# A two-layer decoder step on one core: order of copies and casts, a fourth place for down weights, and the second mixer's norm sum

## The chip, the core and the metric

The kernel runs on one core of a Trainium2 chip. Its time is the device time of one execution in microseconds, as the median of several runs. TensorE multiplies, VectorE and ScalarE do elementwise work and read the accumulators, GpSimd does elementwise work in SBUF, and SyncE issues most transfers from memory.

## The reference, cut to what matters

The reference computes one inference step of two decoder layers, in float32, for 512 prompt tokens and 64 sample tokens that share all weights (576 columns here):

```python
for l in range(2):
    y = mixer(rmsnorm(h, norm_mix[l]))       # layer 0: retention and gMLP; layer 1: windowed attention with sinks
    h = h + y
    h = h + square(relu(rmsnorm(h, norm_mlp[l]) @ w_up[l])) @ w_down[l]
y = rmsnorm(h, norm_final)
```

The width is 1024, that of the MLP 4096. Layer 1's mixer starts with `z = rmsnorm(h) @ w_qkv + b_qkv`: keys and values of 128 rows each, queries of 1024. New caches and states are outputs as well.

## The kernel before, in words

**Layout.** Activations lie transposed: `h[0..7]` are eight tiles of 128 rows by 576 columns. Every float32 product is made of three products of fp32r parts: each operand is split into a high part (a cast on ScalarE, `whi` for weights, line 248) and a low part (a subtraction on VectorE, `wlo`, line 259), and TensorE adds high x high, high x low and low x high in one accumulator. Norm operands are split in the same way (`xhi` line 395, `xlo` line 396). A chunk of 128 output rows is 48 matmuls of 288 columns each (`block`, line 304).

**Weights.** SyncE loads them in pieces of 128 x 1024 floats in a fixed `order`, into three places `raw` (`load_to`, line 215). `jobs` lists what is cast and in which order; `parts` are the finished pairs, for which there are six places (`NW_`). `ahead_to(n)` (line 272) casts until `n` jobs are prepared, and at its end calls `load_to(done + 3)`: three pieces beyond the last one whose casts are all issued.

**MLP.** `rounds_of` (line 434) goes through the 4096 hidden rows in four rounds of eight chunks. The up phase makes eight chunks; their squares are put into a tile `q` in pairs (one place, 128 x 2304 floats), combined there and split into `ahi`, `alo` (lines 475 to 486). The last VectorE instruction that reads `q` is the second subtraction of the fourth pair. The down phase has four *units* (`down_unit`, line 497), m = 0 to 3, each for two tiles of `h`. A unit is a block product with seven multiplications in place of eight (P1 to P7, 12 matmuls each, line 316), so weights are combined first: `s1 = a21 + a22`, `s2 = s1 + a11`, `s3 = a21 + a11`, `s4 = s2 + a12` on VectorE (line 233). A unit's weights are two pieces: `a11, a12` and `a21, a22`. Unit 0 runs P1, P2, P3, P5, P6, P4, P7, the others P1, P5, P6, P2, P7, P3, P4. Results are kept apart by copies on ScalarE: after P1 its bank is copied to `y` before P6 adds to it (line 552), after P6 to `z` (558), after P7 to `w` (565). The last round of the second layer has no units. So there are four rounds with units in the first MLP and three in the second. In the last round of the first, the next norm's operands and squares for finished tiles of `h` are made between the products (`nxt.chunk`, line 387); the squares (ScalarE, line 405) are added up on GpSimd (line 411).

```python
run("P1", x, True)              # takes its weights, multiplies, then ahead_to(used + 5)
y = bank("y")
nc.scalar.copy(out=y, in_=x)
f = bank("f")
run("P5", f, True)
shared(f)
run("P6", x, False)
```

**Order.** VectorE and ScalarE run the MLP in the order in which the program issues it (`manual_schedule`, line 429); elsewhere the compiler orders them. Each engine works through its own queue in order.

**The second mixer** (line 945). The key chunk is multiplied, then `norm.finish()` splits the sum of squares and lets TensorE add it over the partitions (lines 374, 375); the reciprocal root `rstd` scales the key chunk at its evacuation (line 969). The value chunk follows, then eight query chunks. There are two accumulators for chunks.

Of the kernel before, what the change touches and what calls it, by code (L numbers as in the profile page):

```python
# [11 lines left out]
F32 = mybir.dt.float32  # L12
# [6 lines left out]
P = 128  # L19
# [23 lines left out]
NW_ = 6  # L43
# [77 lines left out]
def hybrid_step(ctx: ExitStack, tc: tile.TileContext, a, o):  # L121
# [25 lines left out]
    nc.scalar.activation(out=warm, in_=eps_r, func=AF.Abs_reciprocal_sqrt)  # L147
    cols = keep.tile([P, NCOL], F32, name="cols")
    nc.scalar.dma_start(out=cols, in_=a["cols"])
    h, first = [], []  # L150
    for c in range(KC):
        t = keep.tile([P, T], F32, name=f"h{c}")
# [26 lines left out]


    jobs = [(("left", "right")[j], i) for i in range(len(order)) for j in range(2)]

    def add_pieces(aps):
        for ap in aps:
# [3 lines left out]
    def add_unit(pair, first):  # L188
        jobs.extend((n, len(order)) for n in (FIRST_UNIT if first else UNIT))
        order.extend(pair)  # L190

    def mlp_order(l, last):
        up, dn = a[f"w_up{l}"], a[f"w_dn{l}"]
        for r in range(32 // FB):
            add_pieces([up[r * FB + f] for f in range(FB)])
            if last and r == 32 // FB - 1:
                add_pieces([dn[r, c // 2, c % 2] for c in range(KC)] * 2)
            else:
                for m in range(KC // 2):
                    add_unit([dn[r, m, i] for i in range(2)], m == 0)  # L200

    mlp_order(0, False)
    add_pieces([w_qkv[j] for j in (8, 9, 0, 1, 2, 3, 4, 5, 6, 7)])
    add_pieces([a["w_o1"][c] for c in range(KC)])
    mlp_order(1, True)

    raws, parts, owed = [], [], []
    used, done, summed = [0], [0], [0]
    sums, sum_pool = {}, [None]

# [3 lines left out]

    def load_to(n):
        while len(raws) < min(n, len(order)):
            raw = wp.tile([P, 1024], F32, name="raw", tag="raw", bufs=3)
            nc.sync.dma_start(out=raw, in_=order[len(raws)].rearrange("p k c -> p (k c)"))
            raws.append(raw)

    def blocks_of(i):
        load_to(i + 2)
# [49 lines left out]
    def ahead_to(n):  # L272

        n = min(n, len(jobs))
        while len(parts) < n or owed:
            while summed[0] < min(len(parts) + 2, len(jobs)):
                job, i = jobs[summed[0]]
                k = SUMS.get(job)
                if k:
                    total(k, i)  # L280
                summed[0] += 1
            if len(parts) < n:
                prepare()
            split_low()
        load_to(done[0] + 3)

    def take(n):
        i = used[0]
# [33 lines left out]
    def gemm(xs, outs=None, sides=(0, 1), mid=None, ahead=1):  # L322

        n = len(xs)
        view = None
        if outs is None:
            acc = acc_tile()
            outs, view = [acc[:, hf, 0:TH] for hf in range(2)], acc[:, :, 0:TH]
        got = pieces(n // 8, ahead)
        for k in range(n):  # L330
            for fn in (mid or {}).get(k, ()):
                fn()
            block(outs, cut(got, k), xs[k], sides, k == 0, k == n - 1)
        return view
# [99 lines left out]
    def rounds_of(norm, nxt, mp):  # L434
        rounds = 32 // FB

        def up():

            acc, got = acc_tile(), take(2)
            for k in range(KC):  # L440
                block([acc[:, hf, 0:TH] for hf in range(2)], cut(got, k), norm.xs[k], (0, 1), k == 0, k == KC - 1)
            ahead_to(used[0] + NW_ - 2)
            return acc[:, :, 0:TH]

        def flat(v):
            return v.rearrange("p a b -> p (a b)")

        for r in range(rounds):
            plain = nxt is None and r == rounds - 1
            acts = []  # L450
            for p in range(FB // 2):

                q = mp.tile([P, 8, TH], F32, name="q", tag="q", bufs=1)
                hi = mp.tile([P, 7, TH], F32R, name="ahi", tag="ahi", bufs=FB // 2)
                lo = mp.tile([P, 7, TH], F32R, name="alo", tag="alo", bufs=FB // 2)
                for j in range(2):
                    view = up()
                    if r == 0 and p == 0 and j == 0:
                        norm.finish()
                    t = mp.tile([P, T], F32, name="t", tag="t")  # L460
                    nc.vector.scalar_tensor_tensor(out=halves(t), in0=view, scalar=0.0, in1=norm.rv,  # L461
                                                   op0=ALU.max, op1=ALU.mult)
                    if not plain and p == FB // 2 - 1 and j == 1:
                        ahead_to(used[0] + NW_ - 1)
                    seg = slice(2 * j, 2 * j + 2)
                    nc.scalar.activation(out=flat(q[:, seg]), in_=t, func=AF.Square)  # L466
                    if plain:
                        nc.scalar.activation(out=flat(hi[:, seg]), in_=t, func=AF.Square)  # L468
                        nc.gpsimd.tensor_tensor(out=lo[:, seg], in0=q[:, seg], in1=hi.bitcast(F32)[:, seg],  # L469
                                                op=ALU.subtract)  # L470
                        acts.append((flat(hi[:, seg]), flat(lo[:, seg])))
                if plain:
                    continue

                def two(s0, s1):
                    nc.scalar.copy(out=hi[:, s0 - 1:s1 - 1], in_=q[:, s0:s1])  # L476
                    nc.vector.tensor_tensor(out=lo[:, s0 - 1:s1 - 1], in0=q[:, s0:s1],  # L477
                                            in1=hi.bitcast(F32)[:, s0 - 1:s1 - 1], op=ALU.subtract)

                b12, b11, b22, b21, t1, t2, t3, t4 = (q[:, i] for i in range(8))  # L480
                nc.vector.tensor_tensor(out=t1, in0=b11, in1=b12, op=ALU.subtract)
                nc.vector.scalar_tensor_tensor(out=t2, in0=t1, scalar=-1.0, in1=b22, op0=ALU.mult, op1=ALU.subtract)
                nc.vector.tensor_tensor(out=t3, in0=b22, in1=b12, op=ALU.subtract)
                nc.vector.scalar_tensor_tensor(out=t4, in0=t2, scalar=-1.0, in1=b21, op0=ALU.mult, op1=ALU.subtract)  # L484
                two(1, 4)
                two(4, 8)
                acts.append((hi, lo))
            if plain:
                return [acts[2 * p + j] for j in range(2) for p in range(FB // 2)]
            between = []  # L490
            for m in range(KC // 2):
                down_unit(acts, m, m == 0, between, nxt)
                between = [2 * m, 2 * m + 1] if r == rounds - 1 else []
            for c in between:
                nxt.chunk(c)

    def down_unit(acts, m, first, between, nxt):

# [7 lines left out]
        def bank(name):  # L506
            return m_tile(name)[:, 0:TH]

        def run(n, out, start, stop=True, ks_=range(4), w=None, ahead=NW_ - 1):
            w = w or take(1)[0]  # L510
            product(out, w, lambda k: [t[:, operand[n]] for t in acts[k]], ks_, start, stop, m == KC // 2 - 1)
            if ahead:
                ahead_to(used[0] + ahead)

        def to_h(row, cols_, src, op):
            nc.vector.tensor_tensor(out=row[:, cols_], in0=row[:, cols_], in1=src, op=op)  # L516
# [5 lines left out]
        if first:  # L522
# [24 lines left out]
            to_h(row2, n1, z, ALU.subtract)  # L547
            to_h(row2, n2, z, ALU.subtract)
            return
        run("P1", x, True)  # L550
        y = bank("y")
        nc.scalar.copy(out=y, in_=x)  # L552
        f = bank("f")
        run("P5", f, True)
        shared(f)
# [10 lines left out]
        to_h(row2, n2, z, ALU.subtract)  # L566
        for c in between[1:2]:
            nxt.chunk(c)
        run("P3", x, False)
        to_h(row1, n2, x, ALU.add)  # L570
        run("P4", w_, False)
        to_h(row2, n1, w_, ALU.subtract)

    def last_block(acts, mp):

# [369 lines left out]
    def mixer1(norm, nxt):  # L945
        with tc.tile_pool(name="mx1", bufs=2) as mp:
# [11 lines left out]
            nc.sync.dma_start(out=o["ck_s"][:, 0:W - DL, :], in_=a["cache_k"][:, DL:W, :])  # L958
            nc.sync.dma_start(out=o["cv_s"][:, 0:W - DL, :], in_=a["cache_v"][:, DL:W, :])
            bq = cols[:, COL["b_qkv"]:COL["b_qkv"] + 10]  # L960
            bq8 = mp.tile([P, KC], F32, name="bq8", bufs=1)
            nc.vector.tensor_scalar(out=bq8, in0=bq[:, 0:KC], scalar1=SCALE_S, scalar2=None, op0=ALU.mult)
            xs = norm.xs
            rows_of = [slice(0, 64), slice(64, 128)]

# [3 lines left out]
                nc.vector.tensor_tensor(out=halves(z), in0=view, in1=norm.rv, op=ALU.mult)  # L969
                return z  # L970

            view = gemm(xs)
            norm.finish()
            kT = scaled(view)
            nc.scalar.activation(out=kT, in_=kT, func=AF.Identity, bias=bq[:, 8:9])

            kst = [[w(f"k{part}{kv}", F32R)[:, 0:NP] for part in "hl"] for kv in range(2)]
            for kv, kr in enumerate(rows_of):
                for ds_ in rows_of:
                    nc.scalar.copy(out=kst[kv][0][ds_], in_=kT[kr, 0:NP])  # L980
                own = kst[kv][0].bitcast(F32)
                for ds_ in rows_of:
                    nc.gpsimd.tensor_tensor(out=kst[kv][1][ds_], in0=kT[kr, 0:NP], in1=own[kr], op=ALU.subtract)
            vt = w("vt")[:, 0:NP].rearrange("p (n c) -> p n c", n=NB)
            kvs = mp.tile([NS, 2, P], F32, name="kvs", bufs=1)
            vs = kvs[:, 0, :]
# [21 lines left out]

                later(1, tokens)

            chunk(xs, v_out)


            qs = mp.tile([P, DB, KC, DL], F32, name="qs", bufs=1)
# [332 lines left out]
```

## Time and profile before

| | us |
|---|---|
| median of 3 runs | 1234.64 |
| lowest, highest | 1233.05, 1236.55 |
| the profiled execution | 1236.07 |
| its span, first to last instruction | 1234.0 |
| TensorE busy with matmuls | 1199.2 (97%) |
| VectorE busy | 854.1 (69%) |
| ScalarE busy | 582.3 (47%) |
| GpSimd busy | 192.2 (16%) |
| mean granted clock of TensorE | 0.991 |

Times within the profile count from the span's first instruction. Matmuls are pipelined: one is recorded for about 0.29 us, while in a full stream another starts every 0.13 us. A wait is put down to what released it last. In the rows PE is TensorE's matmuls, DVE VectorE, ACT ScalarE, POOL GpSimd, and SPq SyncE's DMA queue; `out<-in` are the kernel's tiles, and a merged row has a count (x4).

### The profile page before, as it was taken

What the parts mean: (1) busy time and instruction counts of PE and PEld (TensorE: products, weight loads), DVE (VectorE), ACT (ScalarE), POOL (GpSimd) and SP (SyncE); (2) the same over time, 40 slices, a digit from 0 to 9 for tenths busy, and PEclk for the clock granted to TensorE, in tenths of its full rate; (3) what the DMA queues carried; (4) which work ended last, traced back from release to release, by engine and by line L of the source; (5) the groups of instructions that cost most, each with busy time, mean ns of one, the idle gap of its engine ahead of it and who ended that gap; (6) DMA issues with size and microseconds to landing.
All of it is one profiled execution on the core that took longest, in us unless ns stands there. A gap on an engine that the chain in (4) does not pass through costs nothing.

```text
span 1234.0 us, 22717 instructions
## 1 busy us (share of the span) xinstructions
PE 1199.2 (97%) x9213; PEld 1180.0 (96%) x9213; DVE 854.1 (69%) x1546; ACT 582.3 (47%) x1101; POOL 192.2 (16%) x166
## 2 busy tenths in 40 slices
PE   8999999999999999999999999999999999999996
PEld 8999999999999999999999999999999999999996
DVE  8867785456856866875886778546785784784555
ACT  6333454444534444444455777444443443443363
POOL 3543340110000000000014553210000000001223
PEclk9999999999999999999999999899999999999998
DMA  8243222222242233142233212122233233123243
GB/s 281 89 137 122 73 75 83 86 69 72 83 120 70 69 120 86 52 138 69 58 97 110 67 39 67 52 72 71 64 116 90 66 94 113 54 86 120 86 154 111
DMA packets 38521, 113.62 MB, mean 92 GB/s; under 512 B 4161, under 2 KB 11521, under 8 KB 38401
## 3 DMA queue, kind: packets, MB, share of 16 engines
q1 hardware_dynamic: 37408, 110.31, 29.0%
q8 instruction: 72, 1.18, 0.4%
q0 software_dynamic: 320, 1.31, 0.3%
q10 hardware_dynamic: 688, 0.55, 0.2%
q14 instruction: 33, 0.26, 0.1%
HBM read 107.12 MB, written 6.03 MB: 92 GB/s over the span
## 4 chain that ended last, share of the span: by engine, by line
PE 81%; DVE 9%; ACT 3%; DMA 3%; issue 3%; SPq 0%; DVEq 0%; POOL 0%; ACTq 0%
PE acc L304 54%; PE acc L316 7%; PE dn L304 4%; DVE wlo L259 3%; PE w L316 3%; PE f L316 3%; PE y L316 2%; DMA raw<-in_w_dn 2%; PE z L316 2%; DVE h L516 1%; DVE s L233 1%; PE tpp L1093 1%; PE op L1106 1%; PE g L316 1%; ACT whi L248 1%
## 5 line engine op out<-in xcount | busy, mean ns | idle before, releaser
L304 PE MATMUL acc<-xhi,whi 128*128 128x288 f32 x1520 | 325.8, 296 | 0.3 <-DVE vz L708 0.3
L304 PE MATMUL acc<-xlo,whi 128*128 128x288 f32 x1520 | 322.7, 294 | 1.2 <-DVE xlo L396 1.2
L304 PE MATMUL acc<-xhi,wlo 128*128 128x288 f32 x1520 | 323.2, 294 | 0.0
L259 DVE TENSOR_TENSOR wlo<-raw,whi 128x512 fp32r<-128x512 f32 x340 | 250.1, 748 | 92.9 <-ACT whi L248 91.0
L248 ACT CAST whi<-raw 128x512 fp32r<-128x512 f32 x340 | 203.4, 619 | 160.4 <-PE acc L304 110.8
L304 PEld LDWEIGHTS acc<-xlo,whi 128*128 128x128 f32 x1520 | 243.1, 188 | 1.6 <-DVE xlo L396 1.6
L304 PEld LDWEIGHTS acc<-xhi,whi 128*128 128x128 f32 x1520 | 242.1, 188 | 1.8 <-issue 1.3
L304 PEld LDWEIGHTS acc<-xhi,wlo 128*128 128x128 f32 x1520 | 243.5, 188 | 0.3
L466 ACT ACTIVATE q<-t 128x576 f32<-128x576 f32 x64 | 43.9, 686 | 230.9 <-DVE t L461 230.9
L411 POOL TENSOR_TENSOR ssq<-ssq,sq 128x576 f32<-128x576 f32 x25 | 37.2, 1488 | 509.6 <-ACT sq L405 509.4
L461 DVE SCALAR_TENSOR_TENSOR t<-acc,rstd 128x576 f32<-128x576 f32 x64 | 48.4, 756 | 86.0 <-PE acc L304 85.7
L248 ACT CAST whi<-s 128x512 fp32r<-128x512 f32 x112 | 66.1, 620 | 73.4 <-DVE s L233 57.9
L259 DVE TENSOR_TENSOR wlo<-s,whi 128x512 fp32r<-128x512 f32 x112 | 75.7, 686 | 13.5 <-ACT whi L248 13.5
L316 PE MATMUL acc<-ahi,whi 128*128 128x288 f32 x308 | 65.6, 298 | 7.5 <-ACT y L552 7.5
L477 DVE TENSOR_TENSOR alo<-q,ahi 128x864 fp32r<-128x864 f32 (+1 forms) x56 | 67.5, 1205 | 7.2 <-ACT ahi L476 7.2
L316 PE MATMUL acc<-ahi,wlo 128*128 128x288 f32 x308 | 65.0, 296 | 0.0
L316 PE MATMUL acc<-alo,whi 128*128 128x288 f32 x308 | 64.8, 295 | 0.0
L476 ACT CAST ahi<-q 128x864 fp32r<-128x864 f32 (+1 forms) x56 | 58.2, 1039 | 11.9 <-DVE q L484 11.0
L469 POOL TENSOR_TENSOR alo<-q,ahi 128x576 fp32r<-128x576 f32 x8 | 11.5, 1434 | 328.2 <-ACT ahi L468 328.2
L233 DVE TENSOR_TENSOR s<-raw 128x512 f32<-128x512 f32 x56 | 40.9, 730 | 30.4 <-DMA raw<-in_w_dn 30.4
L316 PEld LDWEIGHTS acc<-ahi,whi 128*128 128x128 f32 x308 | 49.0, 189 | 9.3 <-ACT y L552 9.2
L316 PEld LDWEIGHTS acc<-ahi,wlo 128*128 128x128 f32 x308 | 49.1, 189 | 0.0
(323 smaller groups left out, 2213.3 us busy)
## 6 DMA issues: line engine op xcount, KB each, us to landing
raw<-in_w_dn SPq DMA_DIRECT2D x72, 512.0 KB
raw<-in_w_up SPq DMA_DIRECT2D x64, 512.0 KB
raw<-in_w_in SPq DMA_DIRECT2D x22, 512.0 KB
raw<-in_w_o SPq DMA_DIRECT2D x16, 512.0 KB
raw<-in_w_qkv SPq DMA_DIRECT2D x10, 512.0 KB
h<-in_xT SPq DMA_DIRECT2D x8, 288.0 KB
s<-in_s SPq DMA_DIRECT2D x4, 512.0 KB
out_ret_s<-s SPq DMA_DIRECT2D x4, 512.0 KB
```

Of the source, the lines that this page charges most:

```text
L233: nc.vector.tensor_tensor(out=sums[k, i], in0=x, in1=b[y], op=ALU.add)
L248: nc.scalar.copy(out=hi, in_=src)
L259: nc.vector.tensor_tensor(out=lo, in0=src, in1=hi.bitcast(F32), op=ALU.subtract)
L304: nc.tensor.matmul(out, lhsT=w_, rhs=x_[:, hf if isinstance(hf, slice) else half(hf)], start=(start and si == 0), stop=(stop and si == 2))
L316: nc.tensor.matmul(out, lhsT=w[wi][:, k * P:(k + 1) * P], rhs=x(k)[xi], start=(start and n == 0), stop=(stop and n == len(steps) - 1), ski ...
L411: nc.gpsimd.tensor_tensor(out=self.ssq, in0=self.ssq, in1=sq, op=ALU.add)
L461: nc.vector.scalar_tensor_tensor(out=halves(t), in0=view, scalar=0.0, in1=norm.rv, op0=ALU.max, op1=ALU.mult)
L466: nc.scalar.activation(out=flat(q[:, seg]), in_=t, func=AF.Square)
L476: nc.scalar.copy(out=hi[:, s0 - 1:s1 - 1], in_=q[:, s0:s1])
L477: nc.vector.tensor_tensor(out=lo[:, s0 - 1:s1 - 1], in0=q[:, s0:s1], in1=hi.bitcast(F32)[:, s0 - 1:s1 - 1], op=ALU.subtract)
L516: nc.vector.tensor_tensor(out=row[:, cols_], in0=row[:, cols_], in1=src, op=op)
L1093: nc.tensor.transpose(out=tp[:, i * P:(i + 1) * P], in_=s[:, n, hf * P:(hf + 1) * P], identity=ident)
```

## The change

- In unit 1 (m = 1) P1 casts nothing ahead; the copy to `y` follows it, and then `ahead_to(used + 4)`.
- The second piece (`a21, a22`) of units 1 and 3 is loaded into a place with the tag of `q`, so that the three `raw` places hold other pieces. `load_free` replaces `load_to(done + 3)` at the end of `ahead_to`: it loads in order as long as the next piece's place is free, for such a piece only while the down phase is issued (`spare_open`).
- In the last unit of the last round before the second mixer, P3 and P4 cast nothing ahead; the operands of the last two tiles come right behind their updates, then casts, then the two squares.
- In the second mixer the norm's finish and the keys' evacuation and split come in the middle (k = 4) of the value chunk.
- `bq8`, a scaled bias, is made at the start on GpSimd and no longer in the second mixer on VectorE.

```diff
+    bq8 = keep.tile([P, KC], F32, name="bq8")
+    nc.gpsimd.tensor_scalar(out=bq8, in0=cols[:, COL["b_qkv"]:COL["b_qkv"] + KC], scalar1=SCALE_S, scalar2=None,
+                            op0=ALU.mult)
...
                     add_unit([dn[r, m, i] for i in range(2)], m == 0)
+                    if m % 2:
+                        spare.append(len(order) - 1)
...
         while len(raws) < min(n, len(order)):
-            raw = wp.tile([P, 1024], F32, name="raw", tag="raw", bufs=3)
+            if len(raws) in spare:
+                raw = sum_pool[0].tile([P, 1024], F32, name="raw", tag="q", bufs=1)
+            else:
+                raw = wp.tile([P, 1024], F32, name="raw", tag="raw", bufs=3)
...
+    def load_free():
+        while len(raws) < len(order):
+            n = len(raws)
+            if n in spare:
+                free = spare_open[0] and all(i < done[0] for i in spare if i < n)
+            else:
+                same = [i for i in range(n) if i not in spare]
+                free = len(same) < 3 or same[-3] < done[0]
+            if not free:
+                break
+            load_to(n + 1)
...
-        load_to(done[0] + 3)
+        load_free()
...
+            spare_open[0] = True
             for m in range(KC // 2):
                 down_unit(acts, m, m == 0, between, nxt)
                 between = [2 * m, 2 * m + 1] if r == rounds - 1 else []
-            for c in between:
-                nxt.chunk(c)
+            spare_open[0] = False
...
-        run("P1", x, True)
+        run("P1", x, True, ahead=0 if m == 1 else NW_ - 1)
         y = bank("y")
         nc.scalar.copy(out=y, in_=x)
+        if m == 1:
+            ahead_to(used[0] + NW_ - 2)
...
-        run("P3", x, False)
+        if not between or m < KC // 2 - 1:
+            run("P3", x, False)
+            to_h(row1, n2, x, ALU.add)
+            run("P4", w_, False)
+            to_h(row2, n1, w_, ALU.subtract)
+            return
+
+        run("P3", x, False, ahead=0)
         to_h(row1, n2, x, ALU.add)
-        run("P4", w_, False)
+        nxt.operands(2 * m)
+        run("P4", w_, False, ahead=0)
         to_h(row2, n1, w_, ALU.subtract)
+        nxt.operands(2 * m + 1)
+        ahead_to(used[0] + NW_ - 2)
+        for c in (2 * m, 2 * m + 1):
+            nxt.square(c)
+        ahead_to(used[0] + NW_ - 1)
...
-            view = gemm(xs)
-            norm.finish()
-            kT = scaled(view)
-            nc.scalar.activation(out=kT, in_=kT, func=AF.Identity, bias=bq[:, 8:9])
+            kview = gemm(xs)
+            kT = w("z")
...
+            def keys():
+                norm.finish()
+                nc.vector.tensor_tensor(out=halves(kT), in0=kview, in1=norm.rv, op=ALU.mult)
+                nc.scalar.activation(out=kT, in_=kT, func=AF.Identity, bias=bq[:, 8:9])
...
-            chunk(xs, v_out)
+            v_out(gemm(xs, mid={4: [keys]}))
+            stages()
```

## Rows read from the trace of the kernel before

**Rows 1.** The page, part 1: busy us of each engine, share of span, instructions.
```profile
PE 1199.2 (97%) x9213; PEld 1180.0 (96%) x9213; DVE 854.1 (69%) x1546; ACT 582.3 (47%) x1101; POOL 192.2 (16%) x166
```

**Rows 2.** Waits of TensorE, whole span: us in total, times, longest us.
```profile
PE acc L316 <- ACT y L552: 7.5, 7, 1.1
PE w L316 <- ACT w L565: 3.7, 8, 2.0
```

**Rows 3.** Waits of TensorE, 600 to 692 us.
```profile
PE w L316 <- ACT w L565: 2.3, 2, 2.0
PE acc L304 <- DVE xlo L396: 1.2, 2, 0.8
...
PE ms L375 <- DVE sql L213: 0.3, 1, 0.3
```

**Rows 4.** Timeline of ScalarE, 323 to 329 us: start us, us, what [idle before <-releaser].
```profile
324.88 1.14 ACT L248 CAST whi<-s 128x512 fp32r<-128x512 f32 x2 [1.70 <-PE f L316]
```

**Rows 5.** Timeline of TensorE, 318 to 360 us.
```profile
323.02 0.69 PE L316 MATMUL acc<-ahi,wlo 128*128 128x288 f32 x4
...
324.62 0.68 PE L316 MATMUL f<-ahi,wlo 128*128 128x288 f32 x4
326.37 0.80 PE L316 MATMUL acc<-ahi,whi 128*128 128x288 f32 x4 [1.07 <-ACT y L552]
```

**Rows 6.** Timeline of SyncE's DMA queue, around 307 and 318 us.
```profile
307.03 0.33 SPq L218 DMA_DIRECT2D raw<-in_w_dn  x1
...
318.08 0.33 SPq L218 DMA_DIRECT2D raw<-in_w_dn  x1
```

**Rows 7.** Timeline of VectorE, 315 to 330 us.
```profile
315.30 1.36 DVE L477 TENSOR_TENSOR alo<-q,ahi 128x1152 fp32r<-128x1152 f32 x1 [0.26 <-ACT ahi L476]
...
318.69 0.69 DVE L233 TENSOR_TENSOR s<-raw 128x512 f32<-128x512 f32 x1
319.98 0.69 DVE L259 TENSOR_TENSOR wlo<-s,whi 128x512 fp32r<-128x512 f32 x1 [0.60 <-ACT whi L248]
...
321.92 0.69 DVE L259 TENSOR_TENSOR wlo<-raw,whi 128x512 fp32r<-128x512 f32 x1
...
329.65 0.69 DVE L233 TENSOR_TENSOR s<-raw 128x512 f32<-128x512 f32 x1 [1.74 <-DMA raw<-in_w_dn]
```

**Rows 8.** The chain that ended last, in order of time: start us, us, what.
```profile
326.00 3.62 DMA raw<-in_w_dn
...
635.89 3.12 PE w L316 x12
639.01 1.86 PE acc L316 x12
640.87 1.60 PE f L316 x12
```

**Rows 9.** Windows: busy us of PE, PEld, DVE, ACT, POOL; then clock, DMA share, GB/s.
```profile
177.35:181.40 4.05, 4.05 (x32) 4.05 (x32) 2.11 (x5) 1.30 (x2) 0.00 (x0) 1.00 0.62 226
...
637.00:639.10 2.10, 2.10 (x11) 2.10 (x10) 2.10 (x3) 0.63 (x2) 1.42 (x1) 0.50 0.02 4
```

**Rows 10.** Timeline of VectorE in the last round before the second mixer.
```profile
631.65 1.23 DVE L233 TENSOR_TENSOR s<-raw 128x512 f32<-128x512 f32 x1 [1.81 <-DMA raw<-in_w_dn]
```

**Rows 11.** Timeline of VectorE, a lone xlo, then the second mixer's entry.
```profile
621.75 0.81 DVE L396 SCALAR_TENSOR_TENSOR xlo<-h,cols,xhi 128x576 fp32r<-128x576 f32 x1
...
653.66 3.91 DVE L396 SCALAR_TENSOR_TENSOR xlo<-h,cols,xhi 128x576 fp32r<-128x576 f32 x2
...
658.09 0.75 DVE L213 TENSOR_TENSOR sql<-ssq,sqh 128x576 fp32r<-128x576 f32 x1
...
662.83 0.76 DVE L969 TENSOR_TENSOR z<-acc,rstd 128x576 f32<-128x576 f32 x1
...
665.98 0.76 DVE L969 TENSOR_TENSOR z<-acc,rstd 128x576 f32<-128x576 f32 x1 [1.80 <-PE acc L304]
```

**Rows 12.** Timeline of GpSimd at the second mixer's entry.
```profile
653.62 3.32 POOL L411 TENSOR_TENSOR ssq<-ssq,sq 128x576 f32<-128x576 f32 x2 [3.11 <-ACT sq L405]
```

More of the change, by code (lines that the diff above doesn't have):

```diff
@@ L181, in hybrid_step @@
     jobs = [(("left", "right")[j], i) for i in range(len(order)) for j in range(2)]
+    spare = []
     def add_pieces(aps):
@@ L205, in hybrid_step @@
     mlp_order(1, True)
-    raws, parts, owed = [], [], []
+    raws, parts, owed, spare_open = [], [], [], [False]
     used, done, summed = [0], [0], [0]
@@ L960, in mixer1 @@
             bq = cols[:, COL["b_qkv"]:COL["b_qkv"] + 10]
-            bq8 = mp.tile([P, KC], F32, name="bq8", bufs=1)
-            nc.vector.tensor_scalar(out=bq8, in0=bq[:, 0:KC], scalar1=SCALE_S, scalar2=None, op0=ALU.mult)
             xs = norm.xs
@@ L970, in scaled @@
                 return z
-            view = gemm(xs)
-            norm.finish()
-            kT = scaled(view)
-            nc.scalar.activation(out=kT, in_=kT, func=AF.Identity, bias=bq[:, 8:9])
+            kview = gemm(xs)
+            kT = w("z")
             kst = [[w(f"k{part}{kv}", F32R)[:, 0:NP] for part in "hl"] for kv in range(2)]
[L978 to L983, printed above, removed]
+            def keys():
+                norm.finish()
+                nc.vector.tensor_tensor(out=halves(kT), in0=kview, in1=norm.rv, op=ALU.mult)
+                nc.scalar.activation(out=kT, in_=kT, func=AF.Identity, bias=bq[:, 8:9])
+                for kv, kr in enumerate(rows_of):
+                    for ds_ in rows_of:
+                        nc.scalar.copy(out=kst[kv][0][ds_], in_=kT[kr, 0:NP])
+                    own = kst[kv][0].bitcast(F32)
+                    for ds_ in rows_of:
+                        nc.gpsimd.tensor_tensor(out=kst[kv][1][ds_], in0=kT[kr, 0:NP], in1=own[kr], op=ALU.subtract)
             vt = w("vt")[:, 0:NP].rearrange("p (n c) -> p n c", n=NB)
```

## The prediction, made before the changed kernel was run

> **What bounds the kernel now.** I read the page's first part, then the waits of TensorE over the span, then stretch by stretch the waits, the timelines and the chain that ended last. TensorE has an instruction in flight for 1199.2 of 1234.0 us [rows 1], so a change pays only where it takes a wait out of TensorE, or a stretch at the low clock. Two waits of the down phase stand out: 7.5 us in 7 times behind the copy `y` of line 552, and 3.7 us in 8 times behind the copy `w` of line 565, one of these 2.0 us [rows 2]. The long one lies in the last round before the second mixer; behind it come 1.2 us for the last operands `xlo` and 0.3 us for the norm sum [rows 3]. These are all that the change can reach: 7.5 + 3.7 + 1.2 + 0.3 = 12.7 us, and what the clock costs with them. What the reader has to watch is the second-busiest engine. VectorE is busy for 69% of the span [rows 1]; in the down phases it is nearly full and its order is fixed by the program, so whatever makes it stand still there is passed on.
>
> The profiled execution took 1236.07 us (span 1234.0 and 2.07 around it), 1.43 us above the median of 1234.64; I work out a difference in the profile and subtract it from the median.
>
> **1. The copy `y` ahead of its casts** (7 times, unit 1 of every round that has units). Now ScalarE runs two casts from 324.88 for 1.14 us, which had to wait for sums of VectorE, and copies `y` only behind them [rows 4]. TensorE has run P5 to its last four matmuls at 324.62 and then stands 1.07 us, to 326.37 [rows 5]. P1 ends with the four matmuls at 323.02. After the change the copy follows P1 directly, so it can run from about 323.8 to 324.2 beside P5, and P6 could start at about 325.15. Gain 1.07 each, 7.5 us in all. The cover is P5's 1.6 us; the moved casts are needed for P7 and P3, two or more products later, so their lateness has 3 us of cover. Without it a product would start late by the cast's 0.6.
>
> **2. The fourth place for down weights takes something back.** The second half of unit 1 (and of unit 3) is loaded into the tile `q`. Unit 1's load is issued now at 307.03, unit 2's first at 318.08, once unit 0 has given up its second place [rows 6]. The place `q` is free only when VectorE's last subtraction out of `q` has ended, at 315.30 + 1.36 = 316.66 [rows 7], so the load can't be earlier than now, and this part is no gain. A load that is alone takes 3.62 us from the wait's end to its first reader [rows 8], so it lands at 320.3. Two more loads are issued right behind it. Where two loads overlap, 226 GB/s were moved in a stretch of 4.05 us [rows 9]; if two loads of 512 KB shared evenly, 1 MB at that rate is 4.6 us, landing 321.3. So between 320.3 and 321.3; I take 320.6, near the lone load, since the followers come 0.3 us and more later.
>
> The first reader is the sum `s1` at 318.69, and VectorE's queue holds behind it everything the next products need [rows 7]. VectorE has 0.60 us of slack after it (it waits for a cast at 319.98). P1's low part is made at 321.92 + 0.69 = 322.61 and read at 323.02 [rows 5, 7], 0.41 of slack. So TensorE is held up, in P7 of unit 0 and P1 of unit 1 together, by (landing - 318.69 - 0.60 - 0.41) = landing - 319.70: 0.6 at 320.3, 0.9 at 320.6, 1.6 at 321.3.
>
> The Trainium skill (DMA: Bandwidth & Descriptors, § Anatomy of one DMA) gives a DMA a fixed part of about 2.0 us beside its bytes at 436 GB/s; by it 512 KB would be an estimate of 3.2 us and the landing 319.9, a loss of 0.2 only. The trace has 3.62 for the same load, and that is used; that most of it does not shrink with a free place speaks against getting the late start back.
>
> **3. What the places give.** The second half of unit 2 is issued now at the moment its slot's reader is through, 326.00 [rows 8], and VectorE stands 1.74 us for it at 329.65 [rows 7]. After the change it is issued at about 318, when unit 0's second place is given up [rows 6], and the stand goes; likewise in unit 3. VectorE is then 1.3 us later than now from part 2 (320.6 - 318.69 - 0.60) but not 1.74, so some 0.4 us earlier at the copy `w` of unit 1, whose wait is (3.7 - 2.0) / 7 = 0.24. It goes: 0.24 gained. (If the landing is 321.3 it stays.)
>
> An ordinary round, then: 1.07 + 0.24 - 0.9 - 0.1 (a second restart of the matmul stream, four matmuls take 0.80 there against 0.68 [rows 5]) = 0.3 us. Six such rounds: **-1.9 us**.
>
> **4. The last round before the mixer.** VectorE's order is fuller by the operands of the next norm. Its stand of 1.81 us at 631.65 makes the cast and the copy `w` late, and TensorE waits 2.0 [rows 3, 10]. In the stretch after this wait the granted clock is 0.50 [rows 9], the lower of TensorE's two levels (1.2 and 2.4 GHz), so P4 takes 3.12 and the next product 1.86, where one takes 1.60 [rows 8]: 1.52 + 0.26 more. Without the two stands VectorE comes to this place about 2.1 us earlier (1.81 and the 0.3 of part 3). The wait of 2.0 shrinks to some 0.4, and with so short a wait the clock should not fall: 2.0 + 1.8 - 0.4 = 3.4. In unit 3 TensorE has gained more than VectorE, and I allow 0.4 for a late copy there. With the round's own 0.3: **-3.3 us** at the end of the down phase. Bounds: -0.3 if the stand merely moves to another load, -4.4 if nothing is left over.
>
> **5. Operands ahead of weights, and the norm sum mid-chunk.** Now the last two `xlo` take 3.91 us together beside two additions of `ssq` on GpSimd (3.32), where one alone takes 0.81 [rows 11, 12]; TensorE waits 1.2 for them. The Trainium skill (SBUF — State Buffer, § Who interferes with whom) says that a VectorE instruction with two SBUF inputs and a GpSimd instruction that reads SBUF block one another in full. The rows agree; and by this rule the additions, now behind the operands, will block casts of weights instead, so the blocking is moved and not removed.
>
> After the change both `xlo` come before any square. They are ready at about 651.0 and 653.0 (VectorE 2.1 us earlier up to there, then no subtractions of weights between them), against a first need at 651.7 and 652.4 on a TensorE that is 3.3 us earlier: 0.5 us of wait is left of 1.2. But the sum does not come earlier by 3.3. The squares wait for `h`, which VectorE finishes, and the two additions keep their 3.3 us, so the sum's low part, which now is done at 658.09 + 0.75 [rows 11], is done at about 658.2. The value chunk, of 48 matmuls in 6.3 us, ends now at about 665.7 (it is evacuated at 665.98) and has its middle at 662.5; 3.3 us earlier, without 0.7 + 0.3 of waits, the four matmuls of the sum (0.5) and the restarts behind the waits that is 656.9 after the change: a wait of 1.3 us for the low part, where now it is 0.3. From the low part (658.8 now) to the end of the key chunk's evacuation it takes 4.7 us (662.83 + 0.76 [rows 11]), so its accumulator is free at 662.9; the value chunk ends at 661.9, and the first query chunk waits 1.0. Now it waits for nothing and starts at about 665.7, the key chunk having been evacuated 2 us before. So it starts 2.8 us earlier where TensorE entered the mixer 3.3 earlier, **+0.5 us**. Bounds: -1.5 (no wait old or new) and +3 (both new waits longer, on a TensorE that gained all of part 4).
>
> **6. Nothing** is counted for `bq8` on GpSimd: the engine has nothing to do then but constants, hidden behind the first loads; cover gone, it would cost some 0.2 us once.
>
> **Sum.** -1.9 - 3.3 + 0.5 = -4.7 us: 1231.4 in the profile's terms, **1229.9** by the median. About 0.3% (3.7 us) is what a measurement of this kernel can tell from no change.
>
> **The rivals.**
> *A, the place is early enough.* If the load lands by 319.9, an ordinary round gains 1.1: 6 x 1.1 + 3.3 + 0.6 - 0.5 = 10.0, about 1225. For it: everything behind part 1 is sound. Against: from 316.66 it needs 3.2 us where the row has 3.62 [rows 8]. Chance 0.17. (The estimate from the Trainium skill, DMA: Bandwidth & Descriptors, in part 2 would lead here.)
> *B, a wait that takes the place of the one removed.* At a landing of 320.9 to 321.3 an ordinary round costs 0.1 to 0.6 us more, six of them +0.6 to +3.6, and part 4, which starts from the same late sum, gives only -2.5; with the mixer's +0.5 it is 1233 to 1236. For it: the followers on the same 16 engines. The weaker form is that the mixer takes part 4 back whole. Chance 0.29.
> *C, slower.* One mechanism: the load into `q` lands after 322. Then each of seven units stands 2.3 us or more in place of 1.07, and, as after the wait of 2.0 in the last round, the clock falls and costs 1.8 more: 7 x (2.3 + 1.8 - 1.3) = 20 less 3 of part 4, about 1250; with the clock kept, 1239. It decides at a landing of 320.8, where an ordinary round is even, and is over 0.3% at about 321.8. For it: three loads at once. Against: the rate in [rows 9]. Chance 0.11.
> *D, it doesn't do what it says:* the mixer's VectorE and ScalarE are not held to the program's order, so the keys' norm can be placed elsewhere than mid-chunk. That alone is worth -1 to +2 us, and is within the forecast's range.
>
> **Chances.** Forecast 0.43 (1227 to 1233), A 0.17, B 0.29, C 0.11. Of the forecast's case some 0.7 lies beyond -3.7 us, so faster 0.30 + 0.17 + 0.02 = 0.49; within 0.3%: 0.13 + 0.25 = 0.38; slower 0.13, C and the edge of B. Range 1225 to 1237: it takes in A and B and leaves C out.
>
> **What would show it.** Part 1: the 7.5 us behind `y` gone in the list of waits. Part 2: VectorE's `s1` of unit 1 held by a DMA to 320.3 or later, counted from the same point, and new waits of TensorE on `wlo` in P7 and P1; if they are missing, A holds. Part 3: no wait of VectorE for a second half in units 2 and 3. Part 4: no stretch of clock 0.5 in the last round. Part 5: waits of about 1 us each for the sum and for the key chunk's accumulator. The prediction is wrong if an ordinary round is not shorter by 0 to 0.6 us, or the last round with the entry to the mixer by 1 to 4.

## The result, and the profile after

The changed kernel takes **1221.49 us** (median of 4 runs, 1220.70 to 1222.10) against 1234.77 for the kernel before: a ratio of 0.9897, 95% interval 0.9883 to 0.9910, 13.3 us faster. The forecast was 1229.9, 4.7 us faster, with 1225 as the end of its range. The direction was right and the size was not. The profiled execution took 1221.63 us (span 1219.8 and 1.8 around it).

Part 1 of the page after, to be read beside [rows 1]:

```profile
span 1219.8 us, 22708 instructions
...
PE 1194.2 (98%) x9213; PEld 1175.9 (96%) x9213; DVE 852.4 (70%) x1545; ACT 581.9 (48%) x1101; POOL 193.0 (16%) x167
```

Nothing was saved in work: the counts of TensorE are the same. What went is standing still, and time at the low clock. The waits of TensorE over the whole span of after (us in total, times, longest):

```profile
PE ms L397 <- DVE sql L219: 2.7, 3, 1.1
PE tpp L1134 <- ACT pT L1137: 2.4, 1, 2.4
PE acc L326 <- DVE z L1015: 1.7, 1, 1.7
...
PE acc L338 <- ACT y L574: 0.3, 1, 0.3
```

The 7.5 us behind `y` of [rows 2], all in unit 1, are gone; the 0.3 left behind `y` lie in unit 2 of the last round. The 3.7 behind `w` are no longer in the list. New is 1.7 us for the second mixer's key accumulator. The same view from the last round to the attention, answering to [rows 3]:

```profile
PE acc L326 <- DVE z L1015: 1.7, 1, 1.7
PE ms L396 <- ACT sqh L218: 0.5, 1, 0.5
PE ms L397 <- DVE sql L219: 0.4, 1, 0.4
PE acc L338 <- ACT y L574: 0.3, 1, 0.3
```

How late the load into `q` is, was the disputed number. The second round of after, first one step of the chain that ended last in it (start us, us, what):

```profile
413.21 3.51 DMA raw<-in_w_dn
```

VectorE's timeline there, answering to [rows 7]:

```profile
411.82 1.36 DVE L499 TENSOR_TENSOR alo<-q,ahi 128x1152 fp32r<-128x1152 f32 x1 [0.26 <-ACT ahi L498]
...
416.74 0.69 DVE L255 TENSOR_TENSOR s<-raw 128x512 f32<-128x512 f32 x1 [1.42 <-DMA raw<-in_w_dn]
```

TensorE's timeline, answering to [rows 5]:

```profile
417.44 0.70 PE L338 MATMUL z<-alo,whi 128*128 128x288 f32 x4
418.09 0.80 PE L338 MATMUL z<-ahi,wlo 128*128 128x288 f32 x4
418.73 0.70 PE L338 MATMUL acc<-ahi,whi 128*128 128x288 f32 x4
419.26 0.69 PE L338 MATMUL acc<-alo,whi 128*128 128x288 f32 x4
420.02 0.80 PE L338 MATMUL acc<-ahi,wlo 128*128 128x288 f32 x4
```

Four matmuls take 0.53 us from start to start. P7's last four start 0.65 after the four before them and P1's 0.76: hold-ups of 0.12 and 0.23 us, where the kernel before stands 1.07 at `y`. The last subtraction out of `q` ends at 413.18, which is 316.66 in [rows 7], so these rows stand 96.52 later and `s1` starts at 320.22 by the clock of the prediction. What runs beside this load is shown by SyncE's queue:

```profile
403.56 0.33 SPq L227 DMA_DIRECT2D raw<-in_w_dn  x1
413.21 1.73 SPq L227 DMA_DIRECT2D raw<-in_w_dn  x2
423.37 0.33 SPq L227 DMA_DIRECT2D raw<-in_w_dn  x1
```

The load into `q`, for which `s1` waits, is the one issued at 413.21, the fifth of the round's eight; in the program's order it is the fourth. So unit 2's first piece has overtaken it (403.56), and a single load, unit 2's second piece, follows 1.40 us behind. (In the run with the load into the head of `q`, below, the rows name the place: `raw` at 403.02, then `q` at 411.04.) The prediction had both of them right behind the load into `q`.

Where the 14.2 us between the two profiled spans went, by the same matmuls: the six ordinary down phases (from the end of the last up product to the start of the next round's first) are 277.5 us before and 269.6 after, **-7.9**; the last round and the mixer's entry -2.8; the second mixer's attention and output products **-4.9**; some 1.7 us are lost up to the first down phase (of these 1.1 in the first up phase, where the matmuls of after start 133 ns apart and those of before 130), and the rest is below 0.3.

### The profile page after: what moved, and what is told of

Its sections match the earlier page's. It is cut to its first block, busy times and chain, and to the rows that moved or that the text cites. A ratio compares the mean times of both kernels' runs of the same rounds, so it can differ in the third digit from the quotient of the medians.

```text
span 1219.8 us, 22708 instructions
## 1 busy us (share of the span) xinstructions
PE 1194.2 (98%) x9213; PEld 1175.9 (96%) x9213; DVE 852.4 (70%) x1545; ACT 581.9 (48%) x1101; POOL 193.0 (16%) x167
## 4 chain that ended last, share of the span: by engine, by line
PE 82%; DVE 10%; ACT 3%; DMA 2%; issue 2%; POOL 0%; SPq 0%; DVEq 0%; ACTq 0%; POOLq 0%
PE acc L326 54%; PE acc L338 7%; PE dn L326 4%; PE f L338 3%; DVE wlo L281 3%; PE w L338 3%; PE y L338 3%; PE z L338 2%; DMA raw<-in_w_dn 2%; PE op L1147 1%; DVE h L538 1%; PE tpp L1134 1%; DVE alo L499 1%; PE sp L1115 1%; ACT s L1074 1%
```

## The experiments

Medians, and ratios to the kernel before run in the same series on the same chip. The first four rows are one series, the next four a second and the last a third, each on a chip of its own; across series only the ratios compare.

| kernel | us | ratio to before | 95% |
|---|---|---|---|
| part 1 alone (the copy `y`) | 1234.21 | 0.9994 | 0.9982 to 1.0005 |
| the places alone | 1235.83 | 1.0016 | 1.0005 to 1.0027 |
| copy and places | 1226.49 | 0.9929 | 0.9914 to 0.9944 |
| the mixer's entry alone | 1234.80 | 1.0001 | 0.9991 to 1.0011 |
| after, again | 1223.65 | 0.9901 | 0.9883 to 0.9918 |
| after, load into the head of `q` | 1220.88 | 0.9883 | 0.9866 to 0.9899 |
| after, last additions on VectorE | 1222.87 | 0.9899 | 0.9882 to 0.9916 |
| both of these | 1219.07 | 0.9872 | 0.9855 to 0.9889 |
| both, and the keys copied out | 1216.57 | 0.9846 | 0.9822 to 0.9869 |

**Part 1 alone.** The kernel before with

```diff
-        run("P1", x, True)
+        run("P1", x, True, ahead=0 if m == 1 else NW_ - 1)
         y = bank("y")
         nc.scalar.copy(out=y, in_=x)
+        if m == 1:
+            ahead_to(used[0] + NW_ - 2)
```

> The kernel before with part 1 alone: in unit 1 the copy y goes out ahead of the unit's casts; places for weights and the mixer's entry stay as before. Theory (the parts of the down phase need one another): the 7.5 us behind y go, but VectorE still stands some 1.7 us for the second half of units 2 and 3, whose load is issued late, so the copy w becomes late by as much as y was early: an ordinary down phase (46.2 us now from the end of the up products to the next up products) is 45.9 to 46.2, the wait for w grows from 0.2 to about 1.2 a round, the last round keeps its wait of 2 us and more and its stretch at clock 0.50. Time 1232.5 to 1235 against 1234.8. Rival (the copy is worth its own wait): seven rounds of 1.2 us, 8 us, about 1226.5, with the waits for w as they are.

Measured: 1234.21, no difference from before, as the theory has it for the time. The waits of TensorE in its first down phase:

```profile
PE w L316 <- ACT w L568: 1.8, 1, 1.8
```

VectorE's timeline there, the rows that wait for a load:

```profile
329.66 0.69 DVE L233 TENSOR_TENSOR s<-raw 128x512 f32<-128x512 f32 x1 [1.61 <-DMA raw<-in_w_dn]
341.51 0.69 DVE L233 TENSOR_TENSOR s<-raw 128x512 f32<-128x512 f32 x1 [2.95 <-DMA raw<-in_w_dn]
```

TensorE's timeline, the row behind the second of them:

```profile
345.21 1.01 PE L316 MATMUL w<-ahi,whi 128*128 128x288 f32 x4 [1.78 <-ACT w L568]
```

In this phase the wait at `y` is gone and VectorE still stands for the second halves of units 2 and 3; what TensorE gained before them it spends behind them. After this wait of 1.78 the clock was granted at 0.50 for 3.41 us, and the phase took 48.45 us; the other five took 45.8 to 46.05 against 46.2 to 46.35 before, 0.3 to 0.4 each. For the last round the theory was wrong: the wait of 2.0 at `w` did not stay. In its place the profile has 1.2 us at `y` of unit 2 and 1.5 for a low part of weights, and the stretch at clock 0.50 comes behind the wait for `xlo`, at 659.63.

**The places alone.** The kernel before with `spare`, `spare_open`, the tag `q` and `load_free` of the change:

```diff
+            if len(raws) in spare:
+                raw = sum_pool[0].tile([P, 1024], F32, name="raw", tag="q", bufs=1)
...
-        load_to(done[0] + 3)
+        load_free()
```

> The kernel before with the places alone: the second halves of units 1 and 3 go into the tile q; the copy y stays behind its casts and the mixer's entry as before. Theory: the waits for w go (0.4 us a round by the gaps between matmuls), the wait for y stays at 1.07 and takes up the late sum (0.35 more or nothing), so an ordinary down phase is 45.8 to 46.2 instead of 46.2; the last round loses its wait of 2.0 us and its stretch at clock 0.50, 3 to 4 us; the mixer's attention keeps or loses its own falls of the clock. Time 1228 to 1231.5. Rival (the places give the ordinary rounds most of their 1.3 us): 1224 to 1226.

Measured: 1235.83, slower by 0.05 to 0.27%. Both expectations missed. Its waits of TensorE in the first down phase:

```profile
PE acc L335 <- ACT y L573: 1.4, 1, 1.4
```

The same from the last round to the attention:

```profile
PE acc L323 <- DVE xlo L415: 2.2, 2, 1.4
PE acc L335 <- ACT y L573: 1.6, 2, 1.4
```

The late sum holds TensorE up by 0.5 us in P7 and P1 and makes the casts in front of `y` later than TensorE, so that this wait grows from 1.07 to 1.36; with the waits for `w` gone, an ordinary down phase is 46.6 to 46.8, longer by 0.4. The last round loses its wait of 2.0, as expected, but TensorE then waits 2.2 instead of 1.2 for `xlo`, and the stretch at clock 0.50 comes behind that one, at 657.30: from the end of the round's last up product to the same matmul of a query chunk it is 92.4 us for 93.2 before. So part 4 moved into the next wait.

**Copy and places together**, without the mixer's entry: both diffs above.

> The kernel after without the new entry of the mixer (copy y ahead and the places, nothing else). Theory: the ordinary down phases are those of the kernel after, 44.7 to 45.1 us; the entry has its old waits for xlo (1.2 us) in place of the new ones for the sum and the key accumulator (0.9 + 1.7). If the clock falls in the mixer's attention hang on where these stretches lie in time and not on the entry's order, they are gone here too: 1220.5 to 1223. Rival (the new order of the mixer's entry removed them): they stay, 1225 to 1227.5.

Measured: 1226.49. Its waits of TensorE in the first down phase:

```profile
PE z L335 <- DVE wlo L278: 0.2, 1, 0.2
```

The same from the last round to the attention:

```profile
PE acc L323 <- DVE xlo L415: 2.2, 2, 1.4
PE acc L335 <- ACT y L573: 0.3, 1, 0.3
PE z L335 <- DVE wlo L278: 0.2, 1, 0.2
```

Down phases of 45.1 to 45.2, 1.1 us under before. One part alone gains 0.4 a phase, the other loses 0.4, together they gain 1.1: the waits lie one behind the other on VectorE's queue, and with one edit alone the next late thing in it is reached sooner. The falls of the clock stay (651.60, 706.21, 771.07 in the profile), so the theory's 1220.5 to 1223 did not hold. The time is the rival's, 1225 to 1227.5; its reason, that the entry's order removes the falls, does not hold: the kernel after has one too when it is run again (below).

**The mixer's entry alone**, the kernel before with the last two groups of the diff and `bq8`:

> The kernel before with the mixer's part alone: the second mixer's last operands ahead of weights, its norm sum mid-chunk, bq8 on GpSimd; down units as before. Theory: the entry is even to 1 us better (1.2 of waits for xlo go, 0.5 to 1.7 of waits for the sum and the key accumulator come), the wait of 2 us with its clock fall in the last round stays, and so do the falls in the attention: 1233.5 to 1236. Rival (the entry's order is what removed the clock falls of the attention): 1228.5 to 1231.

Measured: 1234.80, no difference. Its waits from the last round to the attention:

```profile
PE w L319 <- ACT w L566: 2.5, 2, 2.0
PE acc L307 <- DVE z L991: 1.7, 1, 1.7
PE acc L319 <- ACT y L553: 1.1, 1, 1.1
PE ms L377 <- ACT sqh L215: 0.5, 1, 0.5
PE ms L378 <- DVE sql L216: 0.4, 1, 0.4
```

The 1.2 us for `xlo` went and 2.6 us came; from the last up product to the same query matmul it is 93.4 us for 93.2. That is not because the new waits cost nothing. The wait of 2.0 in the last round stays, but in this profile no fall of the clock follows it, where all four profiles of before have one ([rows 9] for the first). The same place here (busy us of PE, PEld, DVE, ACT, POOL, then the granted clock, DMA share, GB/s):

```profile
637.65:639.75 2.10, 2.10 (x18) 2.10 (x17) 2.10 (x3) 0.63 (x2) 1.43 (x1) 1.00 0.01 4
```

The last round is 1.2 us shorter for it, and the entry behind it is 1.3 longer. Beside the other parts the entry is worth more: the stretch is 91.2 us without it (copy and places) and 90.4 with it (after), since the long wait for `xlo` and the clock of 0.50 behind it are spared.

**The kernel after again, and the falls of the clock.**

> The kernel after, unchanged, so that the spread of its times and granted clocks stands beside those of the other runs of this call. Theory (the falls of the clock in the second mixer come and go from run to run, as the kernel before has clocks of 0.991 to 0.997 in its runs): the four runs at 0.996 to 0.997 were partly luck; some runs now have 0.993 to 0.995 and are 1.5 to 3 us longer, median 1221 to 1223. Rival (the new order of the mixer's entry keeps the clock up for good): all runs at 0.996 or 0.997, within 1 us of 1221.5.

Measured: 1223.65, three of six runs at a mean clock of 0.995, as the theory has it (one of 1224.1 at 0.997 fits neither); the median lies above the 1221 to 1223 expected. The profiled one has a stretch of 3.41 us at 0.50 from 705.43. What such falls are worth was taken from further profiles of the kernel before:

> The kernel before, unchanged, for one more profile of it. In the runs so far it takes 1233.5 us at a clock of 0.996 and 1236.5 to 1237.5 at 0.991. Theory (between them lie only the falls of the clock): at 0.996 the stretches of clock 0.50 at 636, 711 and 776 us of the first profile are missing, the waits are the same, and the ordinary down phase is 46.2 to 46.4 us as there; the first profile's falls cost 1.8, 1.7 and 3.4 us there, so 6.9 us should be missing. Rival (a run without falls pays elsewhere): only about 3 us are missing, and another stretch is longer by the rest.

> As the run before it: the kernel before, unchanged, a further profile; which of the falls of the clock it has is not known beforehand.

> As the two runs before it: the kernel before, unchanged, a further profile.

Measured: 1237.03 at a mean clock of 0.991, 1232.27 and 1232.78 at 0.996. Windows in the attention of the first profile of before (busy us of PE, PEld, DVE, ACT, POOL, then the granted clock, DMA share, GB/s):

```profile
707.80:710.50 2.70, 0.28 (x3) 0.04 (x1) 1.23 (x4) 2.70 (x12) 2.30 (x3) 1.00 0.00 0
711.15:714.56 3.41, 3.41 (x17) 3.41 (x16) 2.77 (x8) 1.81 (x4) 1.03 (x1) 0.50 0.00 0
776.01:782.84 6.83, 6.83 (x51) 5.99 (x51) 2.23 (x7) 1.83 (x7) 0.00 (x0) 0.50 0.01 2
```

The same places in the second of the three further profiles:

```profile
708.20:710.90 2.70, 0.28 (x4) 0.05 (x2) 1.23 (x4) 2.70 (x12) 2.30 (x3) 1.00 0.00 0
711.15:714.56 3.41, 3.41 (x29) 3.41 (x28) 3.41 (x10) 2.04 (x5) 1.42 (x1) 1.00 0.00 0
776.01:782.84 6.83, 6.83 (x70) 6.29 (x67) 3.97 (x11) 3.40 (x12) 0.00 (x0) 1.00 0.01 2
```

The same kernel stands the same 2.4 us (the line `tpp` in the list of waits, which after has too) and is then granted 0.50 in one execution and 1.00, the full 2.4 GHz, in another. By the starts of the same matmuls the two falls cost 1.5 and 2.9 us. The fall behind the wait of 2.0 us in the last round is in all four profiles of before, though not in that of the mixer's entry alone. So the theory's 6.9 us were too much: 4.4 of them come and go. Against an execution of before without them (1232.27) the profiled one of after (1221.63) is 10.6 us faster, with a first up phase that is 1.1 longer (the last section); where both kernels ran in one series their medians lie 11.8 apart. So the change does some 11 to 12 us. The rest of the first medians' 13.3 can be how often the attention's falls came in the few runs of each; of those runs only two have a profile.

**The load into the head of `q`.** The kernel after, but with

```diff
-                raw = sum_pool[0].tile([P, 1024], F32, name="raw", tag="q", bufs=1)
+                raw = head[0].rearrange("p a b -> p (a b)")[:, 0:1024]      # head[0]: the last q
```

> The kernel after, but the spare weights go into the first 1024 columns of the tile q itself, so that the load waits for the reader of q's first half and not for the last subtraction out of q: it should be issued about 1.3 us earlier. Theory (TensorE's hold-up in P7 of unit 0 and P1 of unit 1 is landing minus 319.70, counted as in the kernel before): the landing moves to about 319, both hold-ups go, with their restarts 0.35 to 0.55 us a round, seven times: down phases of 44.3 to 44.6 us where the kernel after has 44.7 to 45.1, 2.5 to 3.8 us in all. Rival (the load is slowed by the weight loads that are still under way and lands as late as now): within 0.7 us of the kernel after.

Measured: 1220.88, against 1223.65 for after on the same chip. SyncE's queue in the second round:

```profile
411.04 0.33 SPq L228 DMA_DIRECT2D q<-in_w_dn  x1
```

VectorE's timeline there:

```profile
411.27 1.36 DVE L501 TENSOR_TENSOR alo<-q,ahi 128x1152 fp32r<-128x1152 f32 x1 [0.26 <-ACT ahi L500]
...
414.69 0.68 DVE L256 TENSOR_TENSOR s<-q 128x512 f32<-128x512 f32 x1
```

The load is issued 0.23 us ahead of the last subtraction and not behind it, VectorE no longer stands at `s1`, and TensorE's list of waits has no entry in any ordinary down phase: 44.5 us in all six, on the mean 0.4 and 0.55 less than in the two profiles of after. So the rest of the hold-up was the place's lateness alone, as the theory has it.

**The sum's last additions on VectorE.** The kernel after, but with

```diff
-                nc.gpsimd.tensor_tensor(out=self.ssq, in0=self.ssq, in1=sq, op=ALU.add)
+                (nc.vector if vec else nc.gpsimd).tensor_tensor(...)      # vec for the last two squares
```

> The kernel after, but the two last additions of the second mixer's norm sum go on VectorE and not on GpSimd. Theory (what is left at the mixer's entry, 0.45 + 0.40 us for the sum and 1.66 for the key accumulator, hangs on GpSimd's two additions of 3.34 us, which also stretch VectorE's two subtractions beside them to 2.92 us): the sum is ready about 1.5 to 2 us earlier, the waits shrink to 0.5 to 1.0 us in all, 1.5 to 2 us gained, about 1219.7. Rival (VectorE's queue: the additions stand in front of the casts of weights): the waits turn into waits for wlo in the value chunk, 0 to 1 us slower than the kernel after.

Measured: 1222.87, 0.8 us under after in the same series, within the intervals. First, of after, GpSimd's row at the mixer's entry, answering to [rows 12]:

```profile
649.97 3.34 POOL L433 TENSOR_TENSOR ssq<-ssq,sq 128x576 f32<-128x576 f32 x2 [6.09 <-ACT sq L427]
```

VectorE's subtractions of weights beside it, in after:

```profile
650.95 2.92 DVE L281 TENSOR_TENSOR wlo<-raw,whi 128x512 fp32r<-128x512 f32 x2 [0.76 <-ACT whi L270]
```

VectorE's additions and the same two subtractions with the edit:

```profile
650.47 1.61 DVE L433 TENSOR_TENSOR ssq<-ssq,sq 128x576 f32<-128x576 f32 x2
652.00 1.29 DVE L281 TENSOR_TENSOR wlo<-raw,whi 128x512 fp32r<-128x512 f32 x2
```

And its waits of TensorE from the last round to the attention:

```profile
PE acc L326 <- DVE z L1015: 1.6, 1, 1.6
PE acc L338 <- ACT y L574: 0.3, 1, 0.3
```

Half of the theory holds. The waits for the sum are gone, and 1.1 us with them up to the same query matmul (90.4 to 89.3). The wait for the key accumulator has not moved: it is not the sum that is late, but the chain from the sum to the key's multiplication, which starts mid-chunk and is longer than the half chunk that covers it. Without GpSimd's additions beside them, two subtractions of weights take 1.29 us for 2.92; that agrees with the rule weighed in part 5 (the Trainium skill, SBUF — State Buffer, § Who interferes with whom).

**Both edits.**

> Both of the last two edits. Theory: they lie in different stages and add, 4 to 5.8 us under the kernel after, 1216 to 1217.5. Rival (an earlier TensorE reaches the mixer's entry before its operands and gives part of it back): 1218 to 1220.

Measured: 1219.07, 4.6 us under after in the same series. The two gains, 2.8 and 0.8 by the medians, 0.4 to 0.6 a round and 1.1 at the entry by the stretches, add. So the 4 to 5.8 of the theory came; that the time lies in the rival's 1218 to 1220 is because after itself took 1223.65 in this series and not the 1221.5 from which the forecast counted.

**The keys copied out.** Both edits, and the key chunk copied out of its accumulator on ScalarE ahead of the norm:

```diff
             kT = w("z")
+            nc.scalar.copy(out=halves(kT), in_=kview)
...
-                nc.vector.tensor_tensor(out=halves(kT), in0=kview, in1=norm.rv, op=ALU.mult)
+                nc.vector.tensor_tensor(out=halves(kT), in0=halves(kT), in1=norm.rv, op=ALU.mult)
```

> The two edits before (spare weights in the head of q, last two additions of the sum on VectorE) and, new, a copy of the second mixer's key chunk out of its accumulator on ScalarE, ahead of the norm; the multiplication by the norm then reads the copy. Theory (the 1.7 us that the first query chunk waits are the chain from the sum through the reciprocal root to the key's multiplication, 4.6 us against the 3.2 us of half a chunk, and not the sum's lateness): with the accumulator free at about 652 the wait of 1.7 us goes, and its restart; 1.5 to 1.9 us under the kernel without it (1219.1), about 1217.4. Rival (the 0.8 us of the copy delay ScalarE's casts, or the keys are needed at once): the wait returns at the casts of the query chunk or later in the attention, within 0.5 us of 1219.1.

Measured: 1216.57 (5 runs, 1214.70 to 1220.51). All waits of TensorE from the last round to the attention:

```profile
PE tp L1038 <- ACT z L1033: 0.5, 1, 0.5
```

The 1.7 us are gone and 0.5 comes back some 6 us later, behind ScalarE's work on the values; 88.3 us to the same query matmul become 87.2, a gain of 1.1 that lies between the theory's 1.5 to 1.9 and the rival's 0.5. This is the fastest kernel here, 1.3 to 1.8% under before. It ran in another series than the two-edit kernel, and the intervals overlap (0.9855 to 0.9869); the step between them is shown by the stretch, not by the medians.

## Why the prediction was wrong

The forecast was 4.7 us and 11 to 12 came. Nearly all of the error lies in the ordinary down round, which the sum put at 0.3 us and which gave 1.3. The term that failed most is the loss from the late load (part 2).

*What bounds the kernel, and the ceiling.* Right. What the change can reach was put at 12.7 us and what the clock costs with them; 11 to 12 came.

*Part 1, the wait at `y`.* Right in kind: it went in unit 1 of all seven rounds, with P6 behind P5. Its size was the wait's row, 1.07. By [rows 5] the start after the wait comes 1.75 after the start of P5's last four, which take 0.53: 1.22; and the next matmul starts 0.24 later in place of 0.13, so the stall is worth 1.3. The 0.1 for a restart was charged to the change, while the removed stall has one as well.

*Part 2, the late load: the step that failed.* The mechanism stood (the load can't be issued before 316.66, `s1` waits for it, TensorE is held in P7 and P1), but the term for it, 0.9 us a round from a landing of 320.6, was twice too large and more. In the seven rounds of after the load takes 3.2 to 3.6 us, and `s1` starts at 320.0 to 320.4, 320.2 in the middle; with copy and places alone it takes 3.6 to 3.8, and `s1` starts at 320.3 to 320.5. I had added 0.3 to a row of 3.62 for two loads right behind, where a single one follows, 1.3 to 1.4 us later. The prediction's estimate of 3.2 us from the Trainium skill (DMA: Bandwidth & Descriptors, § Anatomy of one DMA) is the lower end of what came in after; that section gives its fit for DMAs that GpSimd issues, and this one is issued by SyncE. The formula, landing less 319.70, gives 0.52 at 320.22 where 0.35 was measured, and with copy and places 0.68 where 0.51 was (the second round of each): the slack behind `s1` is 0.17 larger than the rows gave. So the hold-up is 0.35, and its two restarts 0.2. That the lateness was the whole of this loss is shown by the load into the head of `q`, where it is gone.

*Part 3, the wait for `w`.* It went. Between starts it is 0.3 to 0.5, not 0.24, and 0.1 for the restart.

An ordinary round by these sizes: 1.3 + 0.5 - 0.35 - 0.2 = 1.25 us; measured 7.9 / 6 = 1.3. The forecast had 0.3: 0.55 of the difference is the loss of part 2, 0.2 to 0.3 each are the sizes of the waits at `y` and `w`, and 0.1 goes the other way for the second restart. **These six rounds are 6.0 us of the error**, of the 6 to 7 by which 11 to 12 passes 4.7. Rival A, with 1.1 a round and 1225, had the round right; it asked for a landing by 319.9 and so got a chance of 0.17, where a landing of 320.2 was enough, by the 0.17 of slack and the sizes of the stalls. (By the recorded sum an ordinary round is even at a landing of 320.9; rival C has 320.8.)

*Parts 4 and 5.* -3.3 and +0.5, together -2.8; measured -2.84. That the sum fits is luck: inside, two errors cancel, for the last round gave 4.2 and the entry took 1.3. The waits for the sum were 0.9 together (1.3 said), that for the key accumulator 1.7 (1.0 said); for `xlo` the list has none in this stretch, and between starts it is 0.26 (0.5 said). The fall of the clock that part 4 prices at 1.8 is in all four profiles of before (1.6 in the first by the starts of the matmuls), but the mixer's entry alone had the same wait without the fall. That the two parts must be counted together, because an earlier TensorE meets the next late operand, is what the places alone show.

*Part 6.* `bq8` costs nothing that shows: the wait for `wlf` at the start is 1.3 us in after and 0.5 in the first profile of before, but it is 1.3 in all three later profiles of before and 0.5 in the second of after.

*The attention.* The falls of the clock at 711 and 776 us were in the profile of before and not in the prediction, which looked at one stretch of low clock only. It took that profile's 1236.07 as 1.43 above the median without asking for the cause. They are not something that the change takes out. The first is in a profile of after too. The second is in two of the four profiles of before and in neither of after's two, but it comes back in three of the four variants of after, which all have the new entry. Whether the change makes them rarer is not shown. They move a median of few runs by 2 to 3 us, about half of the forecast itself.

## What to carry to other kernels

Two waits that hang on one engine's queue are not two terms: price each edit with and without the other, since one alone may give nothing or lose. Take a stall's size from the starts of the instructions around it, restart and all, and a transfer's time from the spread of its rows and not from one of them, above all where the sum turns on a few tenths. Where the clock has stretches at its lower level, ask first whether every execution has them.

## What was not expected of the hardware

- The stand of TensorE at 708 us (2.4 us of waiting, matmuls for 0.28 of 2.70 us) is in all fourteen profiles; behind it the granted clock was 0.50 in nine of them and 1.00 in five, for the same kernel too. Behind the wait of 2.0 us in the last round it was 0.50 in the four profiles of before and 1.00 in that of the mixer's entry alone.
- In the first MLP's first up phase the last 336 matmuls take 43.84 us in the eight profiles of the first and third series and the first of before, and 44.96 in the four of the second series and the first of after; in the second MLP 44.95 in all. The granted clock is 1.00 throughout. The cause is open; it puts 1.1 us into a comparison of profiles across series.
- The load into `q` was hardly slowed, if at all, by the one issued 1.3 to 1.4 us behind it: 3.2 to 3.6 us in the seven rounds of after and 3.6 to 3.8 with copy and places, where the one taken for a lone load had 3.62 [rows 8]. No run has it with two loads right behind.
- In every kernel with the mixer's entry part the stretch from the attention's end over the output products is 0.2 to 0.4 us shorter than in profiles of before with the same falls; no run was made to find why.
